# A fourth row buffer for the expert-row gathers, freed by transposing the extra rows' sum back in mid-layer

## The chip, the cores and the metric

The kernel runs on one core of one Trainium2 chip. What counts is the device time in microseconds (us) of one execution, the median of several. Before the change three runs took 2072.07, 2081.8 and 2075.04 us, a median of 2075.04 us.

## The reference, cut to what matters

One inference step of a two-layer decoder: 256 prompt tokens and 32 sample tokens (8 sequences of 4), model width 1024. Each layer is a mixer (an RG-LRU in layer 0, a Conformer convolution in layer 1), a normalisation, and a PEER channel mixer with 16384 experts, followed by another normalisation. The change lies in the PEER part:

```
q = (xb @ w_q).reshape(PEER_BLOCK, N_PEER_HEADS, 2, HALF_KEY)
s = jnp.einsum('thpd,hpnd->thpn', q, keys).astype(jnp.float32)
v1, i1 = lax.top_k(s[:, :, 0], TOPK_HALF)
v2, i2 = lax.top_k(s[:, :, 1], TOPK_HALF)
...
top_s, pos = lax.top_k(cand, TOPK)
expert = jnp.take_along_axis(cand_idx, pos, axis=-1)
g = jax.nn.softmax(top_s, axis=-1).astype(xb.dtype)
u = u_tab[expert]
v = v_tab[expert]
act = jax.nn.gelu(jnp.einsum('td,thkd->thk', xb, u), approximate=False)
return jnp.einsum('thk,thkd->td', g * act, v)
...
x = layer_norm(DEEPNORM_ALPHA * x + g_f * f, p['ln_ffn_g'][i], p['ln_ffn_b'][i])
```

Every token picks 8 x 16 = 128 of the 16384 experts. An expert has a row of `u_tab` and a row of `v_tab`, 1024 numbers each.

## The kernel before

**Two ways to the experts.** For the first 240 prompt tokens the kernel computes all 16384 experts densely: 128 blocks of 128 experts, each with a "u item" (activations, lines 462 to 464) and a "v item" (output, lines 1316 to 1318), both 24 matmuls of 240 columns, since each operand is split into a high and a low part (`wh`, `wl`, lines 233 and 234) and three products are summed. Every item streams 512 KB of weights (tile `raw`, four buffers, issued by SP, line 217). ScalarE (ACT) makes `wh`, VectorE (DVE) makes `wl`; there are three buffers of each. What a token did not pick is multiplied by zero through a gate matrix that DVE and TensorE (PE) build in the background (`gphase`, lines 1231 to 1283).

The other 16 prompt tokens (the "extra" rows, `extra`, line 1389) and the 32 sample tokens (`sample`, line 1428) go by gathers: an indirect DMA, issued by GpSimd (POOL, line 1371), fetches one row of 1024 numbers for each of 128 partitions, 512 KB in all, into a tile `grow`. First comes a u stretch, where DVE multiplies each gathered tile with the token's values and sums along the row (lines 1410 and 1454); then a v stretch, where DVE adds each gathered tile, times the activation, to a sum (`saccx`, line 1423, and `sacd`, line 1467). The extra rows take 16 gathers in each stretch, the sample rows 32.

**The buffers.** All these tiles come from one pool of five 4 KB buffers (tag `g4k`): the gathered rows, the token values `hft`, the sums, and three scratch tiles of the top-16 merge. A gather takes a buffer that has been freed in the order of the program, and waits on the chip until the last reader of that buffer is done. `AH = 2` says how many gathers stand in the program ahead of the use. The sum `saccx` keeps its buffer from the extra v stretch until `peer_end` (line 1472), where eight small matmuls (line 1482) transpose it to the layout of the model's `x` and sum over the heads; eight more (line 1484) do so for `sacd`.

**The order of the work.** It is written out by the program itself: after each item `pump` (line 1096) takes steps of background generators, by an account of PE's time (`tp`) and DVE's (`td`). `bg` holds the top-k and gate work, `bg2` is `extra` followed by `sample`; a generator's `yield` ends a step and gives its price in ns. Each engine then runs its instructions strictly in that order. In layer 0 POOL's queue also loads weights for the next layer's conditioning (line 386, `store<-wada`) among the gathers.

Of the kernel before, what the change touches and what calls it, by code (L numbers as in the profile page):

```python
# [8 lines left out]
F32 = mybir.dt.float32  # L9
# [9 lines left out]
D = 1024  # L19
KT = 8  # L20
NP = 256
ND = 240
XP = NP - ND
NS = 32
N = NP + NS
NB = 8
NL = 4
# [234 lines left out]
class Kern:  # L262
# [170 lines left out]
    def fill(self, gen, n):  # L433
        for _ in range(n):
            next(gen, None)
# [953 lines left out]
    def extra(self, l):  # L1389
        nc, A, wp = self.nc, self.A, self.bp  # L1390
        v = nc.vector
        xin = self.xin
        ei = wp.tile([128, 2, XP], I32, name="xi", tag="xi")
        v.tensor_scalar(ei, xin[:, 0:2], float(l * NE), None, op0=ALU.add)
        yield 100
        hft = self.rows_in(self.hfx)
        act = wp.tile([128, XP], F32, name="xact", tag="xact")
        v.memset(act, 0.0)
        rows = {}
        gather = self.gatherer(ei, rows)  # L1400
        vrows = A["vt"].rearrange("l j i d -> (l j i) d")
        AH = 2
        for c in range(AH):
            gather(A["ur"], 0, c)
        yield 0
        for c in range(XP):
            if c + AH < XP:
                gather(A["ur"], 0, c + AH)
            r = rows.pop((0, c))
            v.scalar_tensor_tensor(r, r, 1.0, hft, op0=ALU.mult, op1=ALU.mult, accum_out=act[:, c:c + 1])  # L1410
            yield 1200
        for c in range(AH):
            gather(vrows, 1, c)
        nc.scalar.activation(act, act, AF.Gelu)
        v.tensor_mul(act, act, xin[:, 2])
        yield 0
        d = self.saccx = self.bp.tile([128, D], F32, name="saccx", tag="g4k", bufs=self.g4b)
        for c in range(XP):
            if c + AH < XP:
                gather(vrows, 1, c + AH)  # L1420
            r = rows.pop((1, c))
            if c:
                v.scalar_tensor_tensor(d, r, act[:, c:c + 1], d, op0=ALU.mult, op1=ALU.add)
            else:
                v.tensor_scalar(d, r, act[:, c:c + 1], None, op0=ALU.mult)
            yield 1200

    def sample(self, l, TKs):
        nc, A, ps, wp = self.nc, self.A, self.ps, self.bp
        v = nc.vector  # L1430
        yield from self.merge(*TKs, 2)
        isel, g = self.sel_out
        ef = wp.tile([128, 2, 32], F32, name="ef", tag="ef")
        ei = wp.tile([128, 2, 32], I32, name="ei", tag="ei")
        for w in range(2):
            v.scalar_tensor_tensor(ef[:, w], isel[:, w].rearrange("p h r -> p (h r)"), 128.0,
                                   isel[:, 1 - w].rearrange("p h r -> p (h r)"), op0=ALU.mult, op1=ALU.add)
            v.tensor_scalar(ei[:, w], ef[:, w], float(l * NE), None, op0=ALU.add)
        yield 400
        hft = self.rows_in(self.hfs)  # L1440
        yield 0
        act = wp.tile([128, 32], F32, name="sact", tag="sact")
        v.memset(act, 0.0)
        rows = {}
        gather = self.gatherer(ei, rows)
        vrows = A["vt"].rearrange("l j i d -> (l j i) d")
        AH = 2
        for c in range(AH):
            gather(A["ur"], 0, c)
        for c in range(32):  # L1450
            if c + AH < 32:
                gather(A["ur"], 0, c + AH)
            r = rows.pop((0, c))
            v.scalar_tensor_tensor(r, r, 1.0, hft, op0=ALU.mult, op1=ALU.mult, accum_out=act[:, c:c + 1])  # L1454
            yield 1200
        for c in range(AH):
            gather(vrows, 1, c)
        nc.scalar.activation(act, act, AF.Gelu)
        v.tensor_mul(act, act, g.rearrange("p h r -> p (h r)"))
        yield 0  # L1460
        d = self.sacc = self.bp.tile([128, D], F32, name="sacd", tag="g4k", bufs=self.g4b)
        for c in range(32):
            if c + AH < 32:
                gather(vrows, 1, c + AH)
            r = rows.pop((1, c))
            if c:
                v.scalar_tensor_tensor(d, r, act[:, c:c + 1], d, op0=ALU.mult, op1=ALU.add)
            else:
                v.tensor_scalar(d, r, act[:, c:c + 1], None, op0=ALU.mult)
            yield 1200  # L1470

    def peer_end(self, l):
        nc, ps, bp = self.nc, self.ps, self.bp
        self.x = self.cp.tile([128, KT, N], F32, name="x", tag="x")
        nc.gpsimd.dma_start(self.x, self.xs)
        flat = self.store.rearrange("p a b -> p (a b)")[:, 6400:6400 + 2 * KT * N]
        zz = flat.rearrange("p (t k n) -> p t k n", t=2, k=KT)
        fill = (lambda n: self.fill(self.fg, n)) if l == 0 else None
        z, zc = zz[:, 0], zz[:, 1]
        pf = ps.tile([128, KT, XP + NS], F32, name="pf", tag="g", bufs=2)  # L1480
        for k in range(KT):
            nc.tensor.matmul(pf[:, k, :XP], self.saccx[:, 128 * k:128 * k + 128], self.selx, start=True, stop=True,
                             skip_group_check=True)
            nc.tensor.matmul(pf[:, k, XP:], self.sacc[:, 128 * k:128 * k + 128], self.sel, start=True, stop=True,
                             skip_group_check=True)
        v = nc.vector
        gate = self.mod[l][:, 40:48]
        v.tensor_mul(z[:, :, ND:NP], pf[:, :, :XP], gate[:, :, 0:1].to_broadcast([128, KT, XP]))
        v.tensor_mul(z[:, :, NP:].rearrange("p k (b l) -> p k b l", l=NL),
                     pf[:, :, XP:].rearrange("p k (b l) -> p k b l", l=NL),  # L1490
                     gate[:, :, 1:9][:, :, :, None].to_broadcast([128, KT, NB, NL]))
        v.tensor_add(z[:, :, ND:], z[:, :, ND:], self.x[:, :, ND:])
        mean = self.ln_begin()
        for p, m in enumerate(VO):
            o = self.vlast(m)
            self.residual_p(z, m, o, l, 40, ND)
            if p == 6 and fill:
                fill(FV)
            if 2 <= p <= PM + 1:
                nc.tensor.matmul(mean, self.ones, z[:, VO[p - 2]], start=p == 2, stop=False)  # L1500
            if p > PM + 1:
                v.tensor_add(self.zsum, self.zsum if p > PM + 2 else z[:, VO[PM]], z[:, VO[p - 1]])
        nc.tensor.matmul(mean, self.ones, self.zsum, start=PM == 0, stop=False)
        nc.tensor.matmul(mean, self.ones, z[:, VO[-1]], start=False, stop=True)
        if l == 0:
            self.ln_mod(mean, z, zc, lambda: self.ln_mod_cols("lnf_g", "lnf_b", 0, 1, 0), 0, fill, 0)
            return
        for k0, k1 in self.ln_norm(mean, z, zc):
            for k in range(k0, k1):
                g, b = self.fv("lnf_g", 8 + k), self.fv("lnf_b", 8 + k)  # L1510
                if k in FT:
                    nc.vector.tensor_scalar(self.x[:, k], zc[:, k], g, b, op0=ALU.mult, op1=ALU.add)
                else:
                    nc.scalar.activation(self.x[:, k], zc[:, k], AF.Identity, scale=g, bias=b)
            nc.sync.dma_start(self.A["yT"][:, k0:k1], self.x[:, k0:k1])
# [23 lines left out]
```

## Time and profile before

| | |
|---|---|
| median of three runs | 2075.04 us (2072.07 to 2081.8) |
| profiled execution, its own time | 2067.63 us |
| its span, first to last instruction | 2065.8 us |
| granted TensorE clock, mean | 0.987 |
| PE busy | 1962.2 us (95%) |
| DVE busy | 1702.2 us (82%) |
| ACT busy | 919.3 us (44%) |
| POOL busy | 367.6 us (18%) |

Layer 0's PEER part ends at about 1032 us, layer 1's at about 2048 us. The stretches of interest, by the trace's times: extra u at 364 to 400 and 498 to 508 us, extra v 516 to 555, sample u 622 to 780 and 872 to 878, sample v 879 to 979 in layer 0; extra v 1541 to 1580, sample u up to 1806 and 1896 to 1902, sample v 1903 to 1995 in layer 1.

A busy PE is not PE at its peak: a matmul's record is about 277 ns long, but they start 112 ns apart, so a short pause between two matmuls disappears under the records' overlap. The number of matmuls in a stretch shows such pauses.

### The profile page before, as it was taken

To read this page: it belongs to the slowest core of one execution; us is meant where nothing else is said; L and a number is where in the kernel's file an instruction comes from. 1 tells how busy PE (TensorE), PEld (TensorE's weight loads), DVE (VectorE), ACT (ScalarE), POOL (GpSimd) and SP (SyncE) were. 2 spreads that over 40 slices of the span, in tenths; PEclk is the share of its full clock that TensorE was granted. 3 is DMA by queue.
4 is the path that set the end of the run, shared out by engine and by line. 5 is a ranking of instruction groups with operands and counts; after the bars stand their busy time and mean duration, and the time that the engine had idled before them with its cause. 6 is when DMAs were issued, how large, how long until landed. Compare 5 with 4: busy or idle time off the path is not lost.

```text
span 2065.8 us, 45941 instructions
## 1 busy us (share of the span) xinstructions
PE 1962.2 (95%) x18898; PEld 1844.5 (89%) x18898; DVE 1702.2 (82%) x3402; ACT 919.3 (44%) x1217; POOL 367.6 (18%) x329
## 2 busy tenths in 40 slices
PE   7998999999999999999988889999999999999997
PEld 3777999999999999988967569999999999999996
DVE  3786899788989989988577478998889889898985
ACT  1855354444444444444452454544444444444443
POOL 1100000401301230155012200013022111401530
PEclk9999999999999999999999899999999999999998
DMA  9766455856867787699569743558578677866992
GB/s 378 248 253 223 144 172 187 315 169 217 315 200 237 258 292 244 213 353 380 189 172 280 265 143 123 184 187 319 172 242 304 201 248 258 305 194 207 352 332 84
DMA packets 135907, 493.86 MB, mean 239 GB/s; under 512 B 16032, under 2 KB 16544, under 8 KB 135056
## 3 DMA queue, kind: packets, MB, share of 16 engines
q1 hardware_dynamic: 93168, 334.09, 49.1%
q0 software_dynamic: 42528, 156.83, 21.4%
q8 instruction: 148, 2.42, 0.5%
q14 instruction: 63, 0.52, 0.1%
HBM read 483.41 MB, written 7.39 MB: 238 GB/s over the span
## 4 chain that ended last, share of the span: by engine, by line
PE 54%; issue 18%; DVE 13%; DMA 8%; POOL 4%; ACT 3%; DVEq 0%; SPq 0%; POOLq 0%; ACTq 0%
PE acc L1317 7%; PE acc L1316 7%; PE acc L1318 7%; PE pu L464 5%; PE pu L462 5%; PE pu L463 5%; DMA grow<-vt,ei 4%; POOL grow L1371 4%; DVE wl L234 3%; PE prj L462 2%; PE prj L464 2%; PE prj L463 2%; PE adap L401 1%; DMA R<-us 1%; PE pd L881 1%
## 5 line engine op out<-in xcount | busy, mean ns | idle before, releaser
L233 ACT CAST wh<-raw 128x1024 fp32r<-128x1024 f32 x583 | 611.3, 1050 | 608.3 <-PE acc L1317 317.3
L234 DVE TENSOR_TENSOR wl<-raw,wh 128x1024 fp32r<-128x1024 f32 x583 | 707.7, 1222 | 126.5 <-ACT wh L233 121.4
L1317 PE MATMUL acc<-gl,wh 128*128 128x240 f32 x2048 | 566.3, 277 | 9.5 <-DVE gl L439 9.2
L464 PE MATMUL pu<-aH,wl 128*128 128x240 f32 x2048 | 565.2, 276 | 9.3 <-DVE wl L234 9.2
L1318 PE MATMUL acc<-gh,wl 128*128 128x240 f32 x2048 | 564.8, 276 | 6.0 <-DVE wl L234 5.9
L1316 PE MATMUL acc<-gh,wh 128*128 128x240 f32 x2048 | 566.9, 277 | 2.3 <-ACT gh L438 2.3
L462 PE MATMUL pu<-aH,wh 128*128 128x240 f32 x2048 | 566.5, 277 | 0.0
L463 PE MATMUL pu<-aL,wh 128*128 128x240 f32 x2048 | 562.9, 275 | 0.0
L1317 PEld LDWEIGHTS acc<-gl,wh 128*128 128x128 f32 x2048 | 388.9, 190 | 13.6 <-DVE gl L439 12.9
L464 PEld LDWEIGHTS pu<-aH,wl 128*128 128x128 f32 x2048 | 389.1, 190 | 12.2 <-DVE wl L234 12.0
L1318 PEld LDWEIGHTS acc<-gh,wl 128*128 128x128 f32 x2048 | 388.7, 190 | 7.8 <-DVE wl L234 7.7
L1316 PEld LDWEIGHTS acc<-gh,wh 128*128 128x128 f32 x2048 | 388.5, 190 | 2.7 <-ACT gh L438 2.7
L463 PEld LDWEIGHTS pu<-aL,wh 128*128 128x128 f32 x2048 | 388.0, 189 | 0.0
L462 PEld LDWEIGHTS pu<-aH,wh 128*128 128x128 f32 x2048 | 387.1, 189 | 0.4 <-issue 0.4
L1339 ACT ACTIVATE store<-pu 128x480 f32<-128x480 f32 x128 | 73.2, 572 | 222.4 <-PE pu L464 218.8
L1371 POOL DMA_INDIRECT grow<-ur,ei x64 | 89.4, 1397 | 382.5 <-DVE grow L1454 268.7
L1371 POOL DMA_INDIRECT grow<-vt,ei x64 | 109.0, 1703 | 189.2 <-DVE grow L1454 111.9
L462 PE MATMUL prj<-aH,wh 128*128 128x288 f32 x392 | 119.5, 305 | 0.0
L1250 DVE TENSOR_TENSOR oA<-c,iT 128x1280 f16<-128x1280 f16 (+1 forms) x136 | 116.8, 859 | 0.0
L463 PE MATMUL prj<-aL,wh 128*128 128x288 f32 x392 | 116.1, 296 | 0.0
L464 PE MATMUL prj<-aH,wl 128*128 128x288 f32 x392 | 115.8, 295 | 0.0
L1281 DVE SCALAR_TENSOR_TENSOR store<-pgt,store 128x460 f32<-128x460 f32 (+3 forms) x184 | 83.6, 500 | 32.8 <-PE pgt L1274 32.5
(360 smaller groups left out, 2671.5 us busy)
## 6 DMA issues: line engine op xcount, KB each, us to landing
raw<-ut SPq DMA_DIRECT2D x256, 512.0 KB
raw<-vt SPq DMA_DIRECT2D x256, 512.0 KB
adaw<-wada POOLq DMA_DIRECT2D x56, 512.0 KB
raw<-w SPq DMA_DIRECT2D x54, 512.0 KB
raw<-wq SPq DMA_DIRECT2D x32, 512.0 KB
adaw<-wada SPq DMA_DIRECT2D x18, 512.0 KB
R<-us POOLq DMA_DIRECT2D x32, 286.5 KB
store<-wada POOLq DMA_DIRECT2D x12, 512.0 KB
```

Source lines behind the costliest of these rows:

```text
L233: nc.scalar.copy(hf, r)
L234: nc.vector.tensor_sub(lf, r, hf.bitcast(F32))
L462: nc.tensor.matmul(pt, h[:, kb], ah[:, ka, n0:n1], start=f, stop=False)
L463: nc.tensor.matmul(pt, h[:, kb], al[:, ka, n0:n1], start=False, stop=False)
L464: nc.tensor.matmul(pt, lo[:, kb], ah[:, ka, n0:n1], start=False, stop=e)
L1250: v.tensor_tensor(a, self.iota2[:, None].to_broadcast([128, g, 128, 2]), bc(0, 128), op=ALU.is_equal)
L1281: v.scalar_tensor_tensor(sv, pg[:, :n, q0 - j0:q1 - j0].rearrange("p t j -> p j t"), 1.0 / 4096.0, sv, op0=ALU.mult, op1=ALU.mult)
L1316: nc.tensor.matmul(o, vh[:, d], wh, start=f, stop=False, skip_group_check=True)
L1317: nc.tensor.matmul(o, vh[:, d], wl, start=False, stop=False, skip_group_check=True)
L1318: nc.tensor.matmul(o, vl[:, d], wh, start=False, stop=e, skip_group_check=True)
L1339: nc.scalar.activation(store[:, s:s + 2], pu[:, :, :ND], AF.Gelu)
L1371: self.nc.gpsimd.indirect_dma_start(out=r, out_offset=None, in_=tab, in_offset=bass.IndirectOffsetOnAxis(ap=ei[:, w, c:c + 1], axis=0))
```

## The change

The extra rows' sum is no longer kept to the end. After the extra v stretch two empty steps pass, then eight matmuls of 16 columns (tile `pfx`, in one of the two buffers of the PSUM tag `g`) transpose it, ACT copies the result to a small tile `xf` of its own, and the sum's buffer is free for the sample stretch. `peer_end` keeps the eight matmuls on `sacd` alone and reads `xf`. Three gathers stand in the program ahead of the use instead of two, in both generators. The account of PE's time is raised by 2000 ns at the place of the eight matmuls.

```
-        AH = 2
+        AH = 3
...
-        d = self.saccx = self.bp.tile([128, D], F32, name="saccx", tag="g4k", bufs=self.g4b)
+        d = self.bp.tile([128, D], F32, name="saccx", tag="g4k", bufs=self.g4b)
...
             yield 1200
+        yield 0
+        yield 0
+        pf = self.ps.tile([128, KT, XP], F32, name="pfx", tag="g", bufs=2)
+        for k in range(KT):
+            nc.tensor.matmul(pf[:, k], d[:, 128 * k:128 * k + 128], self.selx, start=True, stop=True,
+                             skip_group_check=True)
+        self.xf = wp.tile([128, KT, XP], F32, name="xf", tag="xf")
+        nc.scalar.copy(self.xf, pf)
+        self.tp += 2000
+        yield 0
...
-        AH = 2
+        AH = 3
...
-        pf = ps.tile([128, KT, XP + NS], F32, name="pf", tag="g", bufs=2)
+        pf = ps.tile([128, KT, NS], F32, name="pf", tag="g", bufs=2)
         for k in range(KT):
-            nc.tensor.matmul(pf[:, k, :XP], self.saccx[:, 128 * k:128 * k + 128], self.selx, start=True, stop=True,
-                             skip_group_check=True)
-            nc.tensor.matmul(pf[:, k, XP:], self.sacc[:, 128 * k:128 * k + 128], self.sel, start=True, stop=True,
+            nc.tensor.matmul(pf[:, k], self.sacc[:, 128 * k:128 * k + 128], self.sel, start=True, stop=True,
                              skip_group_check=True)
...
-        v.tensor_mul(z[:, :, ND:NP], pf[:, :, :XP], gate[:, :, 0:1].to_broadcast([128, KT, XP]))
+        v.tensor_mul(z[:, :, ND:NP], self.xf, gate[:, :, 0:1].to_broadcast([128, KT, XP]))
```

On PE, at the end of layer 0's extra v stretch, between the last matmuls of a u item (`pu`) and the first of a v item (`acc`); `c_68` is the table of constants that holds the selection matrix. Lines with + are the changed kernel's.

```order
 L463 MATMUL pu<-aL,wh 128x240
 L464 MATMUL pu<-aH,wl 128x240
+L1431 MATMUL pfx<-c_68,saccx 128x16 x8
 L1316 MATMUL acc_5940<-gh,wh 128x240
 L1317 MATMUL acc_5940<-gl,wh 128x240
```

The eight matmuls have moved here from the end of the layer; the order of PE's other matmuls is the same.

On ACT, at the same place; `gh` is the high part of a gate block, `dup` a copy in the sample rows' merge.

```order
 L233 CAST wh<-raw 128x1024 x3
 L1339 ACTIVATE store<-pu 128x480
-L233 CAST wh<-raw 128x1024
-L438 CAST gh<-store 128x480
-L233 CAST wh<-raw 128x1024
+L1434 COPY xf<-pfx 128x128
+L233 CAST wh<-raw 128x1024
+L438 CAST gh<-store 128x480
 L1047 COPY dup<-ix 128x64
 L1048 COPY dup<-ix 128x64
-L233 CAST wh<-raw 128x1024 x2
+L233 CAST wh<-raw 128x1024 x3
```

The copy `xf` stands ahead of the next `wh`, and one `wh` has moved behind the two `dup` copies.

On POOL, layer 0, from the extra gathers (`xi`) to the first gathers of the sample v stretch (`vt,ei`).

```order
 L1371 DMA grow<-ur,xi 128x1024 x16
 L1371 DMA grow<-vt,xi 128x1024 x16
-L1371 DMA grow<-ur,ei 128x1024 x31
+L1371 DMA grow<-ur,ei 128x1024 x32
 L386 DMA store<-wada 128x1024 x6
-L1371 DMA grow<-ur,ei 128x1024
-L1371 DMA grow<-vt,ei 128x1024 x3
+L1371 DMA grow<-vt,ei 128x1024 x4
```

Each sample gather stands one row earlier in the queue; the last one of the u stretch has moved ahead of six loads of conditioning weights.

## Rows read from the trace of the kernel before

**Rows 1.** The page: engines' busy time, then DMA share in 40 slices and rate.
```profile
PE 1962.2 (95%) x18898; PEld 1844.5 (89%) x18898; DVE 1702.2 (82%) x3402; ACT 919.3 (44%) x1217; POOL 367.6 (18%) x329
...
DMA  9766455856867787699569743558578677866992
```

**Rows 2.** Stretches: length, busy us (instructions) by engine, PEclk, DMA share, GB/s.
```profile
520.00:556.00 36.00, 36.00 (x323) 36.00 (x322) 33.34 (x38) 17.37 (x22) 14.72 (x11) 1.00 0.98 367
740.00:780.00 40.00, 37.69 (x363) 37.19 (x362) 32.11 (x43) 17.47 (x21) 18.46 (x13) 1.00 0.91 320
878.00:980.00 102.00, 92.84 (x793) 89.95 (x792) 85.33 (x82) 43.09 (x50) 56.59 (x37) 1.00 0.96 366
1765.00:1806.00 41.00, 40.02 (x389) 39.52 (x388) 34.11 (x46) 18.56 (x22) 19.38 (x14) 1.00 0.93 327
1902.00:1996.00 94.00, 91.10 (x791) 89.27 (x790) 85.16 (x82) 43.11 (x50) 50.87 (x31) 1.00 0.99 363
```

**Rows 3.** Who waited for whom, 878 to 982 us: total us, times, longest.
```profile
DVE sacd L1467 <- DMA grow<-vt,ei: 16.2, 15, 2.7
ACT wh L233 <- DMA raw<-vt: 13.1, 6, 3.8
```

**Rows 4.** Who waited for whom, 1900 to 1998 us.
```profile
DVE sacd L1467 <- DMA grow<-vt,ei: 8.3, 11, 1.9
...
ACT wh L233 <- DMA raw<-vt: 1.9, 1, 1.9
```

**Rows 5.** Timeline of POOL: start, us, instruction, idle before and its releaser.
```profile
540.03 1.68 POOL L1371 DMA_INDIRECT grow<-vt,xi  x1 [0.65 <-DVE saccx L1423]
...
951.12 1.68 POOL L1371 DMA_INDIRECT grow<-vt,ei  x1 [1.14 <-DVE sacd L1467]
```

**Rows 6.** Timeline of DVE around the uses of rows.
```profile
538.48 1.28 DVE L1423 SCALAR_TENSOR_TENSOR saccx<-grow,xact,saccx 128x1024 f32<-128x1024 f32 x1
...
549.24 1.28 DVE L1423 SCALAR_TENSOR_TENSOR saccx<-grow,xact,saccx 128x1024 f32<-128x1024 f32 x1
...
553.90 1.28 DVE L1423 SCALAR_TENSOR_TENSOR saccx<-grow,xact,saccx 128x1024 f32<-128x1024 f32 x1
...
949.57 1.28 DVE L1467 SCALAR_TENSOR_TENSOR sacd<-grow,sact,sacd 128x1024 f32<-128x1024 f32 x1 [0.40 <-DMA grow<-vt,ei]
...
960.03 1.28 DVE L1467 SCALAR_TENSOR_TENSOR sacd<-grow,sact,sacd 128x1024 f32<-128x1024 f32 x1
```

**Rows 7.** Ten-microsecond stretches with the DMA engines full, as rows 2.
```profile
30.00:40.00 10.00, 7.67 (x32) 3.94 (x33) 4.75 (x21) 1.13 (x4) 1.59 (x3) 1.00 1.03 414
...
525.00:535.00 10.00, 10.00 (x91) 10.00 (x91) 9.18 (x9) 4.86 (x6) 5.98 (x4) 1.00 1.02 406
...
945.00:955.00 10.00, 9.45 (x84) 9.23 (x83) 7.12 (x8) 3.66 (x5) 5.32 (x3) 1.00 1.02 396
...
1975.00:1985.00 10.00, 9.96 (x88) 9.76 (x88) 9.45 (x10) 4.89 (x6) 6.20 (x4) 1.00 1.01 374
```

**Rows 8.** Who waited for whom, 740 to 786 us.
```profile
DVE grow L1454 <- DMA grow<-ur,ei: 6.8, 4, 2.5
```

**Rows 9.** Timeline of PE, where `pfx` will stand, and at the layer's end.
```profile
554.25 0.27 PE L1316 MATMUL acc<-gh,wh 128*128 128x240 f32 x1
...
1021.32 0.29 PE L1482 MATMUL pf<-c,saccx 128*128 128x16 f32 x2
...
1024.81 0.36 PE L1316 MATMUL acc<-gh,wh 128*128 128x240 f32 x1
```

**Rows 10.** Timeline of ACT behind the place of `xf`; two copies nearby.
```profile
554.92 1.04 ACT L233 CAST wh<-raw 128x1024 fp32r<-128x1024 f32 x1
...
561.00 0.24 ACT L1047 COPY dup<-ix 128x64 f16<-128x64 f16 x1 [2.92 <-DVE ix L1045]
```

**Rows 11.** Timeline of DVE at layer 0's end, first and last of the residual sums.
```profile
1025.01 0.29 DVE L1488 TENSOR_TENSOR store<-pf,mod 128x128 f32<-128x128 f32 x1 [1.30 <-PE pf L1484]
...
1031.21 0.45 DVE L1502 TENSOR_TENSOR zsum<-zsum,store 128x288 f32<-128x288 f32 x1
```

More of the change, by code (lines that the diff above doesn't have):

```diff
@@ L1487, in peer_end @@
         gate = self.mod[l][:, 40:48]
-        v.tensor_mul(z[:, :, ND:NP], pf[:, :, :XP], gate[:, :, 0:1].to_broadcast([128, KT, XP]))
+        v.tensor_mul(z[:, :, ND:NP], self.xf, gate[:, :, 0:1].to_broadcast([128, KT, XP]))
         v.tensor_mul(z[:, :, NP:].rearrange("p k (b l) -> p k b l", l=NL),
-                     pf[:, :, XP:].rearrange("p k (b l) -> p k b l", l=NL),
+                     pf.rearrange("p k (b l) -> p k b l", l=NL),
                      gate[:, :, 1:9][:, :, :, None].to_broadcast([128, KT, NB, NL]))
```

## The prediction

> **What bounds the kernel now.** I read the page first. PE is busy 95% of the span [rows 1], so a microsecond is won only where PE pauses, and a microsecond of work added to PE is lost. Then I asked the view of stretches for the four places where sample rows are gathered, with the extra v stretch of layer 0 beside them [rows 2]. In that extra stretch PE has no pause: 323 matmuls in 36.00 us, 0.1115 us each. I use that as PE's full rate. In layer 0's sample v stretch there are 793 matmuls in 102 us; at full rate they need 793 x 0.1115 = 88.4 us, so PE stood still for 13.6 us, more than the 9.16 us of idle time that its busy column leaves, because the records overlap. In layer 1's, 791 matmuls in 94 us need 88.2, a stall of 5.8 us. In the dense parts of the two sample u stretches matmuls of several widths are mixed and I take the idle time alone: 40.00 - 37.69 = 2.3 us and 41.00 - 40.02 = 1.0 us. Together 22.7 us of PE time hang on these four places.
>
> The waits say what is late. DVE waits for gathered rows, 16.2 us in layer 0 and 8.3 in layer 1, and ACT waits for the weights of the dense items, 13.1 us and 1.9 us [rows 3, 4]. DVE makes `wl` and `gl` for PE between two rows, in order, so a row that is late holds the next weights back, and PE stops.
>
> Why the row is late shows in who frees the buffer. In layer 0's extra v stretch the gather issued at 540.03 us waits for DVE, and the use that ended just before it started at 538.48 (plus 1.28 is 539.76). That gather's row is the one used at 549.24, the fourth use after that one: four buffers go round. In the sample v stretch the gather of 951.12 follows the use that started at 949.57 and ended at 950.85, and its row is used at 960.03, the third use after it: three buffers go round [rows 5, 6]. So extra already has four buffers, although its program asks for two gathers ahead, and sample has three, since `saccx` keeps the fifth.
>
> **The change part by part.** In extra, three gathers ahead with `hft` or `saccx` and four rows make the same round of four. I cost it at nothing, from -1 to +1 us for both layers, since the order of DVE's and POOL's instructions stays as it is up to the last extra row.
>
> In sample the round grows from three to four. A gather starts one use earlier, some 3.5 us here (949.57 to 960.03 is 10.46 us for three uses). The longest wait of DVE for a row was 2.7 us [rows 3], so every wait would be covered if the transfers themselves could go faster. They can't at will. 366 GB/s x 102 us = 37.3 MB and 363 x 94 = 34.1 MB must move in the two v stretches, and the DMA share is already 0.96 and 0.99 [rows 2]. With the engines full (share 1.01 to 1.03) the rate is 414, 406, 396 and 374 GB/s [rows 7]; leaving out the first, which holds loads of another kind, the mean is 392.
>
> - Layer 0, v: 37.3 MB at 392 GB/s take 95.2 us, 6.8 us less than 102. The bounds are 0 (the rate stays 366) and 13.6 (all stall goes, 422 GB/s, which no row shows). I take 6.5, since the stretch's start isn't full and won't be.
> - Layer 1, v: 34.1 MB at 392 take 87.0 us, less than the 88.2 that PE needs, so PE is the limit and 5.8 could go; at the 374 of this very stretch it is 91.2, a gain of 2.8. I take 4.5, between the two, nearer to the extra v stretch of layer 0, which asks for the same weights and rows per item, has four buffers and shows no pause at 367 GB/s over its whole length.
> - Both u stretches: the DMA share is 0.91 and 0.93, there is room, and DVE waits 6.8 us for rows in layer 0's [rows 8]. Idle PE time is 3.3 us; bounds 0 and 5, the upper end an estimate, since the records' overlap hides some more. I take 2.5, most of what the rows show.
>
> The moved transpose. At the layer's end sixteen matmuls run from 1021.32 to 1024.81, 3.49 us, 0.218 each [rows 9]; eight of them are 1.75 us. DVE's chain at the end starts when they are done, at 1025.01, and runs without a gap to 1031.66 [rows 11], so the end comes 1.75 us earlier, and perhaps 0.2 more because the product with `xf` needn't wait. In mid-layer the same 1.75 us are added to a PE that has no pause there, and a wait with them: PE reaches the place at 554.25, but DVE's last step on `saccx` starts at 553.90 and ends at 555.18 [rows 6, 9], so PE stands 0.9 to 1.0 us. Behind it on ACT, `xf` waits for the matmuls (until about 557.0), and behind `xf` the next `wh`, at 554.92 before [rows 10], some 2.4 us later. Two split items are in hand then, 24 x 0.1115 x 2 = 5.4 us of PE work, which cover it; of the `wh` moved behind `dup`, the same cover is left with 1 to 2 us. The copy itself is taken at the 0.24 us of `dup`. Net per layer: 1.75 + 0.95 - 1.75 - 0.05 = 0.9, for two layers +1.8 us; bounds +0.2 (DVE a step earlier) and +7 (the cover fails and one `wh` is 2.4 late in each layer).
>
> On DVE one pair of `wl` and `gl` comes behind one top-16 step of the sample rows' merge, 1.25 us by the program's own price (line 1038); the cover of 5.4 us hides that too.
>
> The sum: -6.5 - 4.5 - 2.5 + 1.8 = -11.7 us. The profiled execution took 2067.63 us (span 2065.8), so 2055.9 by its clock. The median of the runs is 2075.04, 7.4 us above that execution, and the forecast is made on the median: 2063.3, I say 2063 us. PE is without a pause before and behind these stretches, so what it wins there is not given back.
>
> **The rivals.** *The transfers bind already.* DMA shares of 0.96 and 0.99 [rows 2] speak for it: a fourth gather in flight would only wait longer, and the v stretches would stay as they are. Against it stand 406 and 396 GB/s in ten microseconds of the same work [rows 7]. Then only the u stretches and the transposes count: -2.5 + 1.8 = -0.7, 2074 us. The Trainium skill, in "DMA: Bandwidth & Descriptors", section "Bandwidth", says that about 358 GB/s per core bind for transfers between HBM and SBUF. By that rule 366 and 363 are at the limit and this rival is the outcome; the rates of 374 to 414 in these rows disagree with it, so I hold the rival at less than the forecast.
>
> *All of it goes.* Extra's stretch without a pause speaks for it; against it that layer 0's stretch carries the conditioning loads besides. -13.6 - 5.8 - 3.3 + 1.8 = -20.9, 2054 us.
>
> *Weights pushed back (slower).* In layer 0's v stretch ACT waits 13.1 us for weights, 3.8 at the longest [rows 3]. If the fourth gather is served ahead of a weight load, that load comes one row later, 0.524 MB / 392 GB/s = 1.34 us. It decides once a load's way takes longer than the four weight buffers cover, 4 x 2.68 - 1.04 - 1.22 (`wh`, `wl`) = 8.5 us; then each round of four items is 1.34 longer, and 793 / 24 = 33 items make 8 rounds, 11 us. Layer 0 then turns from -6.5 to +11: +11 - 4.5 - 2.5 + 1.8 = +5.8, 2081 us; if layer 1 goes the same way, 2096. Against it: layer 1 waits 1.9 us for weights. The Trainium skill, same page, section "Queues, rings and completion order", says that each DMA engine takes packets in turn from the queues that have work, which would keep the weights' queue at half the rate whatever the gathers' depth; no row here shows single engines.
>
> *The round stays at three*, if the freed buffer isn't the one that the gathers take. Five buffers less `hft` or `sacd` leave four, so this is unlikely. +1.8 us, 2077.
>
> **How the numbers follow.** Chances: forecast 0.50, transfers bind 0.25, all of it 0.14, weights pushed back 0.07, three buffers 0.04. Some 0.5% (10.4 us) is what a measurement of this kernel can tell from no change, so faster means under 2064.7. Of the forecast (own range 2057 to 2070) about two thirds lie below that, 0.34; with all-of-it 0.48. Slower by over 0.5% is the far half of the weights' rival and a failed cover, 0.05. The rest, 0.47, is the same. Leaving out the weights' rival and the outer ends of the others, the range is 2052 to 2077.
>
> **What would show it.** Right: DVE's waits for `grow<-vt,ei` fall from 16.2 and 8.3 us to a few; sample gathers are freed by the use four before theirs; layer 0's v stretch shrinks to some 95 us at 385 to 395 GB/s, layer 1's to 89 or 90; PE waits about 1 us for `saccx` ahead of `pfx`, and the layer's end starts 1.75 us sooner. Wrong: the v stretches keep their lengths while ACT's waits for `raw` grow (transfers bind, or weights pushed back), or PE waits several microseconds behind `pfx`.

## The result and the profile after

The changed kernel takes 2052.03 us (median of four runs, 2049.53 to 2057.44), the kernel before 2073.56 us beside it (four runs, 2071.0 to 2081.8). The ratio is 0.9897, with a 95% interval of 0.9865 to 0.9928, so the change makes the kernel about 1% faster. The profiled execution took 2049.53 us, 18.1 us less than that of before (2067.63). The forecast was 2063.3, a gain of 11.7 us.

First the page after: the engines' busy time, and the chain that ended last.

```profile
PE 1958.4 (96%) x18898; PEld 1847.7 (90%) x18898; DVE 1702.5 (83%) x3402; ACT 919.2 (45%) x1219; POOL 369.4 (18%) x329
...
PE 74%; DVE 12%; DMA 7%; ACT 3%; issue 3%; POOL 1%; SPq 0%; DVEq 0%; ACTq 0%; POOLq 0%
```

The work is the same as in [rows 1]; PE is a larger share of a shorter span. Where the time went is seen in the stretches of the kernel after: length, busy us (instructions) of PE, PEld, DVE, ACT and POOL, PEclk, DMA share, GB/s. They answer to [rows 2].

```profile
735.00:780.00 45.00, 45.00 (x438) 44.97 (x437) 41.46 (x56) 21.60 (x26) 19.79 (x13) 1.00 0.91 330
877.30:970.30 93.00, 90.34 (x798) 89.58 (x797) 84.92 (x82) 41.74 (x49) 56.34 (x36) 1.00 1.02 400
1745.00:1795.00 50.00, 50.00 (x484) 49.97 (x484) 46.24 (x65) 23.70 (x28) 21.21 (x14) 1.00 0.89 319
1891.50:1979.00 87.50, 87.50 (x781) 87.50 (x781) 85.34 (x82) 42.25 (x49) 50.38 (x30) 1.00 1.01 392
```

Layer 0's sample v stretch now moves 93 x 400 = 37.2 MB in 93 us; before, 37.3 MB took 102 us. Layer 1's moves 34.3 MB in 87.5 us, 781 matmuls at 0.112 us each: PE has no pause left there. In both u stretches PE's busy column is full, and DVE's waits for rows in layer 0's (740 to 785 us, compare [rows 8]) have shrunk to:

```profile
DVE grow L1464 <- DMA grow<-ur,ei: 1.1, 2, 0.8
```

The waits in 876 to 974 us of the kernel after (total us, times, longest), which answer to [rows 3]:

```profile
ACT wh L233 <- DMA raw<-vt: 24.3, 14, 3.0
POOL grow L1371 <- DVE sacd L1477: 24.0, 23, 3.4
ACT wh L233 <- PE acc L1317: 22.7, 17, 2.0
DVE sacd L1477 <- DMA grow<-vt,ei: 7.6, 6, 2.7
```

DVE's waits for rows have halved, 16.2 to 7.6 us; ACT's for weights have grown from 13.1 to 24.3. The transfers are full there (DMA share 1.02); that they are what is left is tested in e6. In layer 1 (1888 to 1984 us) there is no wait of DVE for a row and none of ACT for weights; ACT waits for PE:

```profile
ACT wh L233 <- PE acc L1317: 48.4, 35, 1.7
POOL grow L1371 <- DVE sacd L1477: 22.4, 23, 1.2
```

That four buffers go round shows on POOL's and DVE's timelines (start, us, instruction, idle before and its releaser):

```profile
943.95 1.68 POOL L1371 DMA_INDIRECT grow<-vt,ei  x1 [2.94 <-DVE sacd L1477]
```
```profile
942.39 1.28 DVE L1477 SCALAR_TENSOR_TENSOR sacd<-grow,sact,sacd 128x1024 f32<-128x1024 f32 x1 [2.19 <-DMA grow<-vt,ei]
...
953.70 1.28 DVE L1477 SCALAR_TENSOR_TENSOR sacd<-grow,sact,sacd 128x1024 f32<-128x1024 f32 x1
```

The gather of 943.95 follows the use that ended at 942.39 + 1.28 = 943.67; its row is used at 953.70, the fourth use after that one (the third in [rows 5, 6]).

The last place is mid-layer, PE's timeline and the stretch around it:

```profile
552.53 0.28 PE L464 MATMUL pu<-aH,wl 128*128 128x240 f32 x1
553.63 1.96 PE L1431 MATMUL pfx<-c,saccx 128*128 128x16 f32 x16 [0.82 <-DVE saccx L1423]
555.43 0.36 PE L1316 MATMUL acc<-gh,wh 128*128 128x240 f32 x1
...
557.05 0.41 PE L1318 MATMUL acc<-gh,wl 128*128 128x240 f32 x1
557.27 0.41 PE L1316 MATMUL acc<-gh,wh 128*128 128x240 f32 x1
```
```profile
553.00:560.00 7.00, 6.37 (x42) 6.38 (x43) 5.84 (x33) 2.62 (x7) 0.00 (x0) 0.76 0.40 111
```

PE waits 0.82 us for `saccx`, as forecast, and does the eight matmuls in 1.80 us. But then matmuls start 0.22 us apart instead of 0.112: from 556.40 on the granted clock is 0.5, that is 1.2 GHz in place of 2.4. This was not in the prediction. Layer 1 shows the same at 1570.16.

To put the time to places, the start of the same `wh` cast on ACT was taken in both traces; the table has how much the difference (after less before) grew in each stretch. "Forecast" is the prediction's term; all are rounded.

| stretch | forecast | measured |
|---|---|---|
| start to 525 us, extra u and most of extra v | 0 | -1.6 |
| mid-layer 0, with the transpose | +2.7 | +4.5 |
| sample u, layer 0 | -2.5 with layer 1 | -3.5 |
| sample v, layer 0 | -6.5 | -9.5 |
| end of layer 0 | -1.8 | -1.6 |
| mixer of layer 1, to 1549 us of before | 0 | -0.7 |
| mid-layer 1 | +2.7 | +4.5 |
| sample u, layer 1 | (above) | -2.6 |
| sample v of layer 1 and its end | -6.3 | -7.5 |
| sum | -11.7 | -18.1 |

Two rows can't be put down to the change. Up to the moved matmuls e1 and e2 (below) ask for two gathers ahead as the kernel before does, and their first row reads -3.1 and -1.1 us; in two profiles of one kernel (e6, e11) it reads -5.4 and -2.4. The mixer's row scatters more (e8). The other rows, the places of the change, sum to -15.8 us.

The mixer's row also hides a loss: of the 1.6 us won at layer 0's end 1.5 are given back by 1055 us of before's time, as the granted clock falls to 0.5 at 1037.7 us of the kernel after. A fall at this place is in e1, e2 and e5 too and in no other profile; why is not shown. The place in the kernel after, then its surroundings in before:

```profile
1038.00:1040.00 2.00, 2.00 (x10) 2.00 (x10) 1.81 (x4) 1.71 (x4) 0.00 (x0) 0.50 0.00 0
```
```profile
1030.00:1060.00 30.00, 25.11 (x161) 16.92 (x161) 22.89 (x61) 20.33 (x32) 2.16 (x3) 1.00 0.21 67
```

### The profile page after: what moved, and what is told of

Its sections match the earlier page's. It is cut to its first block, busy times and chain, and to the rows that moved or that the text cites. A ratio compares the mean times of both kernels' runs of the same rounds, so it can differ in the third digit from the quotient of the medians.

```text
span 2047.7 us, 45928 instructions
## 1 busy us (share of the span) xinstructions
PE 1958.4 (96%) x18898; PEld 1847.7 (90%) x18898; DVE 1702.5 (83%) x3402; ACT 919.2 (45%) x1219; POOL 369.4 (18%) x329
## 4 chain that ended last, share of the span: by engine, by line
PE 74%; DVE 12%; DMA 7%; ACT 3%; issue 3%; POOL 1%; SPq 0%; DVEq 0%; ACTq 0%; POOLq 0%
PE acc L1316 10%; PE acc L1317 10%; PE acc L1318 10%; PE pu L464 9%; PE pu L462 9%; PE pu L463 9%; DVE wl L234 3%; DMA grow<-vt,ei 3%; PE prj L462 2%; PE prj L464 2%; PE prj L463 2%; PE pgt L1274 2%; PE pgt L1272 2%; PE adap L401 1%; PE prj L471 1%
## 5 line engine op out<-in xcount | busy, mean ns | idle before, releaser
L1281 DVE SCALAR_TENSOR_TENSOR store<-pgt,store 128x460 f32<-128x460 f32 (+3 forms) x184 | 83.9, 501 | 34.3 <-PE pgt L1274 33.9
```

Source lines behind the costliest of these rows:

```text
L1281: v.scalar_tensor_tensor(sv, pg[:, :n, q0 - j0:q1 - j0].rearrange("p t j -> p j t"), 1.0 / 4096.0, sv, op0=ALU.mult, op1=ALU.mult)
```

## The experiments

Kernels of one round share their runs of the kernel before, which had a median of 2071.45 us beside e1 to e4, 2068.41 beside e5 to e8, and 2072.09 beside e9 to e11. Totals of one kernel scatter by 10 us and more (why is told under e8), so the verdicts below rest on the stretches. "Step" is the growth of the difference to before, taken as in the table.

**e1: two gathers ahead.** Edit, in both generators of the changed kernel:

```
-        AH = 3
+        AH = 2
```

> The changed kernel with two gathers ahead in the program instead of three, in both generators; the transpose stays in mid-layer, so the freed buffer stays free. Theory (the buffers decide): a gather waits for the last reader of its buffer, and with five buffers less hft or sacd four go round whatever the program asks for, as in the extra stretch of the kernel before. Then sample gathers follow the use four before theirs, 0.28 us after its end, and the time is that of the changed kernel, 2052 us, within 4. One gather of layer 0 stands behind six loads of conditioning weights again, which may cost 1 us at the border of sample u and v. Rival (the three ahead decide): the sample gathers fall back to the use three before theirs, the gain of the sample stretches goes, and what is left is the cost of the moved transpose: 2075 us or more.

Measured: 2051.34 us (ratio 0.9917, 0.9886 to 0.9947). Step of layer 0's sample v -9.5, as in the changed kernel. POOL's and DVE's timelines of this kernel:

```profile
942.25 1.68 POOL L1371 DMA_INDIRECT grow<-vt,ei  x1 [0.87 <-DVE sacd L1477]
```
```profile
940.70 1.28 DVE L1477 SCALAR_TENSOR_TENSOR sacd<-grow,sact,sacd 128x1024 f32<-128x1024 f32 x1
...
951.94 1.28 DVE L1477 SCALAR_TENSOR_TENSOR sacd<-grow,sact,sacd 128x1024 f32<-128x1024 f32 x1
```

The gather follows the use of 940.70, and its row is the fourth after it, as with three ahead. The freed buffer is all of the gain; the number three adds nothing that can be seen.

**e2: the move alone.** The changed kernel with `AH = 2`, and in `peer_end` a reader that holds the buffer:

```
-        d = self.bp.tile([128, D], F32, name="saccx", ...)
+        d = self.saccx = self.bp.tile([128, D], F32, name="saccx", ...)
...
+        hold = bp.tile([128, 1], F32, name="hold", tag="hold")
+        nc.scalar.copy(hold, self.saccx[:, :1])
```

> The moved transpose alone: two gathers ahead, and the buffer of saccx is held to the layer's end by a copy of one column there, so that three rows go round in the sample stretches as before. Theory (the move costs a pause and a stretch at half clock): +4.5 us in the middle of each layer less 1.6 at its end, for two layers +5.8, 2079 us against 2073.6 of the kernel before; PE waits about 0.8 us for saccx, and a few microseconds of granted clock 0.5 follow within 1 us of the eight matmuls in both layers. Rival 1 (as forecast): the pause and the matmuls alone, +1.8, 2075 us, no half clock there in this kernel. Rival 2 (the new order itself brings the gain, not the buffer): below 2065 us.

Measured: 2077.8 us against 2071.45, ratio 1.0023 (1.0002 to 1.0044), so by the ratio +4.8 us where the theory had +5.8 and the forecast +1.8. The steps in mid-layer are +4.5 and +4.7, of the four sample stretches +0.2, +0.7, +1.2 and +1.1; there each gather again follows the use three before its own. Mid-layer 0 and 1 of this kernel:

```profile
553.50:560.50 7.00, 6.30 (x42) 6.30 (x43) 5.92 (x33) 2.88 (x7) 0.00 (x0) 0.77 0.48 117
1585.00:1592.00 7.00, 6.48 (x43) 6.48 (x44) 5.74 (x33) 2.37 (x7) 0.00 (x0) 0.76 0.45 119
```

The move brings nothing by itself, and each mid-layer loses clock. Rival 2 falls. The forecast's +1.8 lies inside the interval (+0.4 to +9.1 us), so rival 1 falls by the steps and the clock, not by the total.

**e3: the transpose one item later.** Edit:

```
         yield 0
         yield 0
+        yield 700
         pf = self.ps.tile([128, KT, XP], F32, name="pfx", tag="g", bufs=2)
```

> The changed kernel with one priced step of 700 ns ahead of the eight matmuls on saccx, which puts them one v item (24 matmuls, 2.7 us of PE) later; the sample rows' merge moves with them. Theory (the pause takes the clock down): PE finds saccx done, waits 0.1 us or less, and no half clock follows: 0.8 and 1.7 us less in each layer, 5 us in all, 2047 us. Rival 1 (the eight matmuls of 16 columns themselves take the clock down): the pause goes, the half clock stays, -1.6 us, 2050. Rival 2 (the weights behind the copy xf become late): PE waits for wh after the moved matmuls, 2052 us or more.

Measured: 2050.79 us (ratio 0.9891, 0.9859 to 0.9924). PE's timeline and the two mid-layers:

```profile
554.06 0.28 PE L1318 MATMUL acc<-gh,wl 128*128 128x240 f32 x1
554.17 1.85 PE L1432 MATMUL pfx<-c,saccx 128*128 128x16 f32 x16
555.88 0.36 PE L1316 MATMUL acc<-gh,wh 128*128 128x240 f32 x1
```
```profile
553.00:560.00 7.00, 7.00 (x65) 7.00 (x65) 5.30 (x31) 3.02 (x7) 0.00 (x0) 1.00 0.44 140
1572.00:1579.00 7.00, 7.00 (x65) 7.00 (x64) 4.90 (x31) 3.01 (x7) 0.00 (x0) 1.00 0.47 154
```

No wait for `saccx`, no half clock; the step is 1.79 us in each layer instead of 4.50, and the matmuls alone are that. So 5.4 us are won at the two places, as the theory has it, and both rivals fall: the half clock goes with the pause, and PE has no pause behind the matmuls (65 in 7 us). The total doesn't show it: in this run layer 1's mixer took 4.9 us longer than in before, and layer 0's sample v gained 7.7 instead of 9.5.

**e4: six buffers, transpose left at the end.** Edit of the kernel before (with `AH = 3`):

```
-                    self.g4b = 5
+                    self.g4b = 6
```

> The kernel before with six buffers of 4 KB instead of five and three gathers ahead; the transpose stays at the layer's end. Four rows go round in the sample stretches and five in the extra ones. Theory (the row buffers bring all of the gain, the move only costs): the gain of 21.5 us plus the 5.8 that the move costs, 2073.6 - 27.3 = 2046 us; no half clock and no pause of PE at 553 to 560 and 1566 to 1575 us. Rival 1 (PE's pauses in mid-layer are won back later, since the transfers set the pace): 2052 us, as the changed kernel. Rival 2 (part of the gain comes from the order that the move brings): 2056 us or more.

Measured: 2043.17 us (ratio 0.9874, 0.9842 to 0.9906); sample steps -3.5, -10.5, -2.6, -5.5, no pause and no half clock in mid-layer. What is left in layer 0 (876 to 972 us: the stretch, and the waits):

```profile
876.00:972.00 96.00, 94.05 (x833) 93.47 (x832) 87.01 (x83) 44.66 (x52) 52.61 (x33) 1.00 1.01 395
```
```profile
ACT wh L233 <- DMA raw<-vt: 28.9, 18, 2.8
...
DVE sacd L1467 <- DMA grow<-vt,ei: 6.6, 6, 1.9
```

The gain comes without the move, so it is the buffer's.

**e5: the changed kernel again**, unedited.

> The changed kernel once more, beside the kernels that follow, since single runs of one kernel lie up to 20 us apart. Both theories expect 2052 us, within 4; its stages should start at the same offsets from the kernel before as in its first profile (mid-layer +4.5 us per layer).

Measured: 2050.44 us (ratio 0.9915, 0.9893 to 0.9938). The two mid-layers:

```profile
552.00:559.00 7.00, 6.18 (x56) 5.99 (x55) 5.96 (x29) 2.28 (x4) 0.00 (x0) 1.00 0.46 146
1571.00:1578.00 7.00, 6.18 (x41) 5.99 (x40) 5.93 (x33) 2.67 (x6) 0.00 (x0) 0.76 0.51 135
```

An expectation that missed: in layer 0 the clock stayed at 1.00 this once, and the step was 2.87 us, close to the forecast's 2.7; in layer 1 it fell, and the step was 4.49. The difference, 1.6 us, is the price of the half clock.

**e6: six buffers, conditioning loads later.** Edit of e4's kernel:

```
-ADJ = (52, 56, 60, 66, 70, 74, 78, 82, 92, 96, 98, 102, 104)
+ADJ = (52, 56, 60, 66, 70, 74, 108, 110, 112, 114, 116, 118, 120)
```

> The kernel before with six buffers, three gathers ahead, and the last six loads of conditioning weights of layer 0 (6 x 0.524 = 3.1 MB) taken at later items, behind the sample v stretch. Theory (in layer 0 the transfers are what is left: DMA share 1.01 at 395 GB/s, ACT waits 28.9 us for weights): 3.1 MB / 395 GB/s = 8 us less to transfer in this stretch, so PE's stall of 96 - 833 x 0.1115 = 3.1 us goes: 2040 us against 2043 with the loads among the gathers, and ACT's waits for raw<-vt in 868 to 970 us fall below 10 us. Rival 1 (the stall is DVE's, which makes wl and gl between rows): the waits for weights change little, 2043 us. Rival 2 (the loads, now late, hold up the layer's end or the beginning of layer 1): more than 2046 us, PE waits for store<-wada behind 1020 us.

Measured: 2040.28 us (ratio 0.9865, 0.9842 to 0.9887). Layer 0's sample v, and its waits in 868 to 970 us:

```profile
876.00:972.00 96.00, 96.00 (x858) 96.00 (x857) 86.12 (x83) 45.48 (x54) 51.53 (x34) 1.00 1.01 392
```
```profile
ACT wh L233 <- DMA raw<-vt: 6.2, 4, 2.0
...
DVE sacd L1467 <- DMA grow<-vt,ei: 1.5, 2, 0.9
```

PE has no pause left; 858 matmuls instead of 833. The step of the stretch is -13.2 us, and it is -13.2 in e10 and e11 too: then PE is the limit. What was left in layer 0 was the transfers, and the loads among them. Rival 1 falls; of rival 2 nothing is seen here, PE waits for no `store<-wada` in 1020 to 1060 us (but see e11).

**e7: six buffers, four gathers ahead, the transpose one item later** (the edits of e3 and e4 on the changed kernel, with `AH = 4`).

> The changed kernel with six buffers, four gathers ahead and the transpose one item later: five rows go round in the sample stretches. Theory (four rows already cover the way of a row; what is left in layer 0 is transfer): no more is won than by four rows, layer 0's sample v stretch within 1 us of that of the kernel with six buffers and no move; +1.8 us in each mid-layer and -1.6 at each end, 2043 to 2046 us. Rival 1 (a fifth row wins more): layer 0's stretch shrinks by another 2 to 3 us, 2041 us. Rival 2 (a deeper ring pushes the weights back): ACT's waits for raw<-vt grow beyond 35 us, 2050 us or more.

Measured: 2042.08 us (ratio 0.9868, 0.9845 to 0.9892). Step of layer 0's sample v -11.9, 1.5 beyond e4 and 2.5 beyond e8; of layer 1's the same -5.5. The stretch:

```profile
876.00:972.00 96.00, 95.83 (x846) 95.09 (x845) 88.44 (x84) 45.25 (x53) 50.45 (x33) 1.00 1.01 393
```

The theory's "within 1 us" missed: in this one profile a fifth row takes some of layer 0's last stall, at the same rate of transfer (the most with four rows and the loads in place is -10.7, in e5). In layer 1 nothing was left to take. Five rows also did not push the weights back: ACT waits 13.3 us for them in 876 to 974.

**e8: six buffers again**, e4's kernel unedited.

> The kernel before with six buffers and three gathers ahead, once more beside the others: 2043 us within 4, 9 us less than the changed kernel in the same round of runs. Rival (its first time was luck of the runs): within 4 us of the changed kernel.

Measured: 2048.4 us (ratio 0.9897, 0.9875 to 0.9919), against 2043.17 the first time and 2050.44 of the changed kernel beside it. By the number set down ahead the rival holds: 2 us, not 9. The stretches say what differs: the sample steps are as in e4 (-3.5, -9.4, -2.6, -5.5), but at layer 0's end the clock fell during the sixteen matmuls, as it had not in e4. That stretch in e4, then in e8:

```profile
1005.00:1015.00 10.00, 8.83 (x78) 8.64 (x78) 7.66 (x18) 2.12 (x2) 0.00 (x0) 1.00 0.34 109
```
```profile
1005.00:1015.00 10.00, 10.00 (x62) 10.00 (x61) 5.55 (x12) 1.33 (x2) 0.00 (x0) 0.66 0.30 99
```

The step there is +3.2 us. In e6 and e11, which also have all sixteen matmuls at the end, the clock falls behind them too, for +1.6 us each; their 1000 to 1010 us:

```profile
1000.00:1010.00 10.00, 9.97 (x74) 9.78 (x73) 6.70 (x15) 1.65 (x2) 0.00 (x0) 0.83 0.31 105
1000.00:1010.00 10.00, 10.00 (x78) 10.00 (x77) 4.94 (x8) 2.99 (x3) 0.00 (x0) 0.83 0.47 162
```

So the place at the layer's end has its own risk; right behind the eight matmuls that the move leaves there the clock fell in no profile. The rest is mostly layer 1's mixer (1036 to 1240 us of before), whose duration against before differs between two profiles of one kernel: -1.4 and +3.0 us (e4, e8), -1.4 and +7.0 (e6, e11), -0.4 and +4.4 (the changed kernel, e5). No order between the kernels can be read from single runs. By totals, six buffers without the move are ahead of the changed kernel in e4's round and not to be told from it in e8's.

**e9: one matmul of the eight.** Edit of the changed kernel (the copy repeats the one block):

```
-        for k in range(KT):
+        for k in range(1):
```

> The changed kernel with one of the eight matmuls on saccx in mid-layer (the other seven are left out, and the copy repeats the first block), so that PE has the pause and nearly nothing of the small matmuls. The pause with all eight was followed by granted clock 0.5 in 7 of the 8 places recorded so far, the eight without a pause in none of 4. If the pause alone takes the clock down: 0.5 within 2 us of the place in both layers, a step of 1.0 + 0.2 + 1.7 = 2.9 us at each. If it takes the pause and the small matmuls together: clock 1.0 behind the place, a step of 1.0 + 0.2 = 1.2 us.

Measured: 2046.42 us (two runs). PE's timeline and the two mid-layers:

```profile
554.61 0.40 PE L1431 MATMUL pfx<-c,saccx 128*128 128x16 f32 x2 [0.82 <-DVE saccx L1423]
```
```profile
553.00:560.00 7.00, 6.18 (x55) 5.98 (x55) 6.72 (x34) 3.25 (x7) 0.00 (x0) 1.00 0.56 169
1567.00:1574.00 7.00, 6.18 (x55) 5.99 (x55) 6.32 (x34) 3.66 (x8) 0.00 (x0) 1.00 0.50 174
```

The same pause, clock 1.00 at both, a step of 1.31 us each. The pause alone does not take the clock down here; pause and eight small matmuls did at 7 of 8 places; the eight without a pause at none of 6 (e3, e7, e10).

**e10: five buffers, the transpose one item later, the loads later** (the edits of e3 and e6 on the changed kernel).

> The changed kernel, five buffers, with the transpose one v item later and the last six loads of conditioning weights of layer 0 behind the sample v stretch. Theory (two separate costs are left in the changed kernel, the pause in mid-layer and the loads beside the gathers): 2.7 us less in each mid-layer, and PE's stall of about 3 us in layer 0's sample v goes: -8.4 us, 2042 us against 2050.4; no PE idle in 876 to 972 us. Rival (the place of the transpose and the loads work on the same slack, or the late loads disturb the layer's end): 2047 us or more.

Measured: 2041.71 us (ratio 0.9850, 0.9827 to 0.9873), 8.7 us less than e5's median where the theory had 8.4, though in another round of runs; the interval of its ratio doesn't meet e5's, but touches that of the changed kernel's first runs (0.9865 to 0.9928). Mid-layer steps 1.79 and 1.79, layer 0's sample v -13.2:

```profile
876.00:972.00 96.00, 96.00 (x858) 96.00 (x857) 90.10 (x86) 46.14 (x54) 53.27 (x36) 1.00 1.01 395
```

It beats the changed kernel with the same memory. By the stretches the two costs are separate.

**e11: e6's kernel again**, unedited.

> The kernel before with six buffers and the six loads behind the sample v stretch, once more beside the others: 2040 us within 4, the fastest so far. Rival (half clock at layer 0's end or in layer 1's mixer, which differs from run to run, decides): 2046 us or more, with the sample stretches as in its first profile.

Measured: 2045.52 us (ratio 0.9868, 0.9843 to 0.9893). The sample steps are those of its first profile within 0.1 us; layer 1's mixer took 7.0 us longer than before's, where it had been 1.4 shorter. In e10 it took 6.9 longer; these are the two longest of all the profiles, and both kernels have the late loads. Since e6 has them as well, whether the loads have a part in it is open. The median of e11 lies between the two expectations. Whether it or e10 is faster stays open.

## Why the prediction was right, and where its sizes were off

**How far it was right.** The direction held, and so did the mechanism below. The total held barely: 2052.03 us lies 0.03 us inside the recorded range (2052 to 2077) and below the forecast's own range (2057 to 2070). Medians of one kernel lie up to 5 us apart (e4 and e8, e6 and e11), so on which side of that edge it fell was luck. The gain is 21.5 us in medians and 18.1 in profiles, since the profiled execution of before was 5.9 us under its median and that of after 2.5; in e5 the medians are 18.0 apart. At the places of the change it is 15.8, against a forecast of 11.7.

**The mechanism held.** The diagnosis from [rows 5, 6], three buffers round in sample and four in extra, and the step to four: e1 shows the round, e2 that without the freed buffer nothing is won, e4 that the buffer wins it without the move. "The round stays at three" and "transfers bind already" are out. "Weights pushed back" is half seen: ACT does wait longer for weights in layer 0, but the stretch still gets shorter.

**Sample v, layer 0: the rate of transfer was mis-sized.** Forecast -6.5, measured -9.5 (-7.7 to -10.7 over seven profiles with a round of four and the loads in place). The step "37.3 MB at 392 GB/s" took the mean of three ten-microsecond stretches as what can be kept up; the stretch as a whole ran at 400. The same bytes at 400 take 93 us, 9 less than before. The Trainium skill, "HBM Reference", section "Specifications (TRN2)", says that a core that streams alone measures well above the share of 358 GB/s, about 425. The trace agrees, with 400 GB/s over 93 us, short of the 425; the rule of 358 that the prediction weighed does not hold for this single core.

**Sample u: idle time read from the busy column was too little.** Forecast -2.5 for both layers with an upper end of 5, measured -6.2. The prediction had seen that records overlap and hide pauses, yet took the busy column here (2.3 and 1.0 us), since widths are mixed. The waits showed that more was there: DVE waited 6.8 us for rows in layer 0 [rows 8] and now waits 1.1, and PE won 3.5 us, between the idle time and the waits.

**Sample v and end of layer 1.** Forecast -6.3, measured -7.5, 5.5 of it in the stretch: PE is the limit, as "5.8 could go" had it; the shading to 4.5 was too careful.

**The moved transpose: a term was missing.** Pause and matmuls came as computed (0.82 and 1.80 us, with the forecast's 0.95 and 1.75), and `xf` held up nothing. The half clock behind them, 1.6 us at most places, was not thought of: +4.5 per mid-layer instead of +2.7. At 1.6 us in each layer that is some 3.3 us that the kernel could still gain, and 5.4 with the pause (e3).

**In sum**, against the forecast layer 0's sample v gave 3.0 us more, the two sample u 3.7, layer 1's sample v with its end 1.2, the table's first row and layer 1's mixer, which are scatter, 2.3; layer 0's end gave 0.2 less (and 1.5 went again in the mixer), and the move cost 3.6 more at its new places. So -11.7 became -18.1 in the profiles. The outcome lies next to the recorded rival "all of it goes" (2054 us), but not by its reason in layer 0: there all of it went only when the loads were moved too (e6, e10).

## What to carry to other kernels

Ask of a ring of buffers how many go round on the chip, by which use frees the next transfer, rather than how many the program asks for; one buffer more in a stretch where the use waits for the row was worth some 21 us here (the four sample stretches), against 5.8 that the move which freed it cost. A small piece of work that is moved into a full engine costs its length, the wait for its input, and possibly the clock behind it: place it one item later than seems needed. When kernels differ by less than the scatter of their runs, compare the same instruction's start stage by stage, and profile one kernel twice to see which stages scatter by themselves.

## What the runs showed of the hardware that was not expected

- After 0.8 to 1.0 us without work and eight matmuls of 16 columns (1.80 us), PE's granted clock fell to 0.5 at 7 of 8 places, and cost 1.6 us; with the pause and one matmul at none of 2, with the eight and no pause at none of 6. Sixteen in a row (16 and 32 columns, 3.5 us) behind full work, without a pause, stand at the layers' ends of before, e4, e6, e8 and e11: there it fell during them or within 1.1 us behind them at 6 of 10 places. Behind the eight of 32 columns that the other kernels keep there it fell as soon at none of 16. The same kernel at the same place can go either way (after and e5, e4 and e8).
- The transfers of one core kept 400 GB/s over 93 us, gathered rows and weights together.
- Layer 1's mixer, where the clock falls several times in each profile, differs by up to 8.4 us between two profiles of one kernel (e6 and e11, whose profiled spans are 9.4 us apart). Its granted clock in 1060 to 1240 us was 0.95 and 0.91 there, and PE's wait for one transfer (`R<-us`, between 1000 and 1245 us) 5.7 and 13.2 us; which of them makes the difference is not shown.
